# Layer 1's operands on VectorE in a fixed order, half its first values ahead of them, and flips two blocks ahead

## The chip, the cores and the metric

One core of a Trainium2 chip runs the kernel. The metric is the device time of one execution in microseconds, the median of the runs. TensorE (PE) multiplies, VectorE (DVE), ScalarE (ACT) and GpSimd (POOL) do the rest, SyncE (SP) issues the loads and stores.

## The reference

A trunk of two layers on 1024 tokens of width 1024, in float32, with pre-RMSNorm and residual adds. Layer 0 has global, windowed and memory heads; layer 1, which the change touches, is this:

```python
h = rmsnorm(x, norm_gain[l])
qc, kc, vc, qm, gate = split_cols(h @ w_in_odd[o], SPLIT_ODD)   # 1024, 1024, 1024, 512, 1536 columns
yc = neighborhood_attn(qc, kc, vc, rpb_c[o])    # 16 heads of 64; 8 x 16 window on the token grid
ym = memory_attn(qm, mk, mv)                    # 4 heads of 128; 256 memory tokens
y = jnp.concatenate([yc, ym], axis=-1) * jax.nn.silu(gate)
x = x + y @ w_out_odd[o]
```

## The kernel before

All large products run in a split form: each float32 operand is a high part and a low part (`x - high`), and a product is three matmuls (high-high, low-high, high-low). ScalarE copies out high parts, VectorE or GpSimd subtract to get low parts. Weights come by DMA into `wraw`, and `w_parts` (L1050) makes `wh` and `wl`. `either()` lets weights' low parts alternate between VectorE and GpSimd.

The stages follow each other in one program: preparation and layer 0, its output projection `out0`, then `front`, then layer 1's memory heads, its eight pairs of near heads, and `out1`. `front` (L1203) computes seven pairs of layer 1's projection columns (gates and memory queries) ahead. It uses a Strassen form: seven products of 12 matmuls of 128x512 for each pair of column tiles, 588 matmuls. Four of the seven need operands made of sums of blocks of the activations, `t1` to `t4` (4 tiles each, high and low). The half of the tokens that `out0` finishes last (`b12`, `b22`) is normalised inside the front: squares are summed in `out0` (`square`, L1111, GpSimd adding them through the tile `bt`), the sum goes through `rstd_cols` (matmuls L256, a chain of small VectorE operations, L229 to L234) and four flips (TensorE transposes) to one row per token, and VectorE scales `P` and `yb` tiles (L1243). The differences of L1226 and the low parts of L1228 and L1233 are shared between VectorE and GpSimd. For the weights, `sums` (L1336) makes four sums for each pair on GpSimd (VectorE for one pair). A pair's first two products are x (`begin`) and z (`second`); `finish` adds them, and `end` applies tanh for a gate. Five pairs start early, so x and z fill time while operands are made.

The order on each engine comes from a scheduler that runs through the program; `ahead(kind)` moves an operation up by the amount in `AHEAD`, `issue_after` holds one behind another, and `keep_in_program_order` pins VectorE's order for those operations that are marked.

In layer 1, `values` (L348) computes V for one half of the heads (8 head columns, group g) as a generator: 24 matmuls of 128x512 for each of 8 token blocks, in pieces of 12. `pull(n)` takes n pieces from the waiting generators and puts them between other work. Two such generators fill the memory heads (`mem_att`). In `near_head` (L922), a loop over 8 token blocks makes scores (L959, L960), the exponent and its normalisation (ScalarE L971 or GpSimd L973), and `values(j)` with flips (L110) and the products with V (L942); between flips and products it pulls `pulls` pieces of projection for the next pair (L215). The last pairs' gates are computed lazily, too, and `gated` (L389) multiplies a head's rows by them on GpSimd.

## Time and profile before

| | us |
|---|---|
| runs | 1574.67, 1576.52, 1577.83; median 1576.52 |
| profiled execution | 1580.0, of which the span from first to last instruction 1578.2 |
| busy: TensorE | 1502.0 (95%) |
| busy: VectorE, ScalarE, GpSimd | 1049.4, 838.6, 779.8 |
| front (first to last of its products) | 811.17 to 975.08 |
| memory heads with value matmuls | 987 to 1112 |
| near heads | 1130 to about 1440 |

The page's share for TensorE is a mean over stages. What a stage can lose is read in windows on it: its length less TensorE's busy time is idle time, and PEclk under 1.00 is time at the lower clock. A wait row names the tile that TensorE wanted and the engine that wrote it last. A "busy" matmul of 512 columns shows 0.39 us, but the next one starts 0.23 us later; the prices here go from start to start.

### The profile page before, as it was taken

What the parts mean: (1) busy time and instruction counts of PE and PEld (TensorE: products, weight loads), DVE (VectorE), ACT (ScalarE), POOL (GpSimd) and SP (SyncE); (2) the same over time, 40 slices, a digit from 0 to 9 for tenths busy, and PEclk for the clock granted to TensorE, in tenths of its full rate; (3) what the DMA queues carried; (4) which work ended last, traced back from release to release, by engine and by line L of the source; (5) the groups of instructions that cost most, each with busy time, mean ns of one, the idle gap of its engine ahead of it and who ended that gap; (6) DMA issues with size and microseconds to landing.
All of it is one profiled execution on the core that took longest, in us unless ns stands there. A gap on an engine that the chain in (4) does not pass through costs nothing. (4 is left out here: it accounts for less than half of the span.)

```text
span 1578.2 us, 24720 instructions
## 1 busy us (share of the span) xinstructions
PE 1502.0 (95%) x8082; PEld 1279.5 (81%) x8082; DVE 1049.4 (66%) x2210; ACT 838.6 (53%) x1890; POOL 779.8 (49%) x870
## 2 busy tenths in 40 slices
PE   6999999999999999999995999999999999998997
PEld 5899888888888788878874788877788888887786
DVE  7768677777776578766569654443477777776654
ACT  7644566556655456655445444343366666655442
POOL 2523455546563645432477654223266666643354
PEclk8999999999999999999998999999999999999998
DMA  9535332233232313387640344575556566767834
GB/s 349 181 102 159 98 103 102 66 129 101 83 125 75 126 65 107 100 277 243 195 167 34 134 160 150 177 239 174 169 180 185 176 201 203 221 188 264 272 119 135
DMA packets 163744, 249.83 MB, mean 158 GB/s; under 512 B 13856, under 2 KB 96032, under 8 KB 162592
## 3 DMA queue, kind: packets, MB, share of 16 engines
q1 hardware_dynamic: 162752, 247.52, 47.9%
q8 instruction: 64, 1.05, 0.3%
q10 hardware_dynamic: 864, 0.74, 0.2%
q14 instruction: 64, 0.52, 0.1%
HBM read 164.32 MB, written 74.45 MB: 151 GB/s over the span
## 5 line engine op out<-in xcount | busy, mean ns | idle before, releaser
L215 PE MATMUL pj<-H,wh 128*128 128x512 f32 x1248 | 418.4, 416 | 0.6 <-DVE vt L286 0.4
L102 ACT ACTIVATE ph<-tr 128x512 fp32r<-128x512 f32 (+2 forms) x336 | 180.6, 541 | 150.5 <-PE tr L110 144.5
L426 DVE TENSOR_TENSOR pl<-tr,ph 128x512 fp32r<-128x512 f32 (+2 forms) x336 | 205.7, 615 | 67.2 <-ACT ph L102 64.6
L215 PE MATMUL pj<-H,wl 128*128 128x512 f32 x624 | 247.9, 397 | 0.0
L215 PEld LDWEIGHTS pj<-H,wh 128*128 128x128 f32 x1248 | 215.0, 191 | 32.9 <-PE sa L560 0.8
L215 PEld LDWEIGHTS pj<-H,wl 128*128 128x128 f32 x624 | 118.0, 189 | 28.4
L1054 POOL TENSOR_TENSOR wl<-wraw,wh 128x384 fp32r<-128x384 f32 (+1 forms) x69 | 81.4, 1182 | 118.8 <-ACT wh L102 104.0
L102 ACT ACTIVATE wh<-wraw 128x384 fp32r<-128x384 f32 (+1 forms) x155 | 84.0, 549 | 92.0 <-PE tr L1100 17.3
L133 POOL TENSOR_TENSOR wl<-wraw,wh 128x512 fp32r<-128x512 f32 x86 | 112.1, 1306 | 22.0 <-ACT wh L102 14.5
L973 POOL TENSOR_SCALAR pn<-pn,st 128x384 f32<-128x384 f32 (+1 forms) x128 | 76.8, 602 | 90.8 <-DVE st L972 53.4
L110 PE MATMUL tr<-ident,P 128*128 128x128 f32 x752 | 117.5, 275 | 1.9 <-POOL P L583 1.8
L132 POOL TENSOR_SCALAR wh<-wraw 128x512 fp32r<-128x512 f32 x86 | 56.4, 656 | 123.5 <-PE pj L215 92.8
L880 POOL TENSOR_SCALAR P<-P,st 128x1024 f32<-128x1024 f32 x64 | 75.8, 1186 | 67.1 <-DVE st L879 67.0
L110 PEld LDWEIGHTS tr<-ident,P 128*128 128x128 f32 x752 | 90.4, 141 | 10.4 <-POOL P L583 3.0
L971 ACT ACTIVATE pn<-pn,st 128x384 f32<-128x384 f32 (+1 forms) x128 | 74.8, 585 | 36.2 <-DVE st L970 30.5
L878 ACT ACTIVATE P<-sa,st 128x1024 f32<-128x1024 f32 x64 | 71.5, 1118 | 41.6 <-DVE st L877 24.6
L877 DVE TENSOR_REDUCE st<-sa 128x1 f32<-128x1024 f32 x64 | 77.6, 1219 | 13.0 <-PE sa L873 11.9
L365 PE MATMUL pj<-k,H 128*128 128x512 f32 x256 | 84.4, 398 | 0.3 <-DVE ph L373 0.3
L702 PE MATMUL pj<-ah,H 128*128 128x256 f32 x384 | 72.9, 286 | 0.0
L110 PE MATMUL tr<-ident,pn 128*128 128x128 f32 x352 | 66.9, 275 | 4.9 <-POOL pn L973 4.4
L583 POOL TENSOR_SCALAR P<-P,st 128x384 f32<-128x384 f32 (+1 forms) x64 | 38.9, 625 | 59.9 <-DVE st L578 54.6
L967 DVE CUSTOM_DVE_ANT_0 pn<-s,bm 128x384 f32<-128x384 f32 x96 | 52.3, 555 | 22.6 <-PE s L960 10.0
(456 smaller groups left out, 4061.7 us busy)
## 6 DMA issues: line engine op xcount, KB each, us to landing
wraw<-w_o SPq DMA_DIRECT2D x62, 256.0 KB, 4.0
y<-sg SPq DMA_DIRECT2D x24, 512.0 KB, 2.9
y<-yb SPq DMA_DIRECT2D x24, 512.0 KB, 3.2
wraw<-s SPq DMA_DIRECT2D x64, 192.0 KB, 3.3
wraw<-w_e SPq DMA_DIRECT2D x44, 256.0 KB, 2.9
k<-k SPq DMA_DIRECT2D x36, 256.0 KB, 3.9
wraw<-w_mem SPq DMA_DIRECT2D x32, 256.0 KB, 4.4
v<-ph SPq DMA_DIRECT2D x32, 256.0 KB, 2.2
```

The source lines that it names most:

```text
L102: return self.nc.scalar.activation(out, in_, AF.Copy, scale=scale)
L110: self.turned = self.fence = self.nc.tensor.transpose(o, i, self.ident)
L133: (nc.gpsimd if self.wsplit[1] == "pool" else nc.vector).tensor_tensor(lf, raw, hf, op=OP.subtract)
L215: nc.tensor.matmul(a[:, :n], s[:, kt % UNIT, :], m, start=(kt == 0 and i == 0), stop=(kt == KT - 1 and i == 2))
L365: nc.tensor.matmul(p, x[kt][:, t], m, start=(kt + i == 0), stop=(kt == KT - 1 and i == 2))
L426: nc.vector.tensor_tensor(pl[:, :n], tr[:, :n], ph[:, :n], op=OP.subtract)
L702: self.last = nc.tensor.matmul(a[:, b * 256:(b + 1) * 256], x[kt][:, t], w, start=(kt + b + i == 0), stop=(kt == KT - 1 and i == 2), skip_ ...
L877: nc.vector.tensor_reduce(st[:, 0:1], s, axis=AX.X, op=OP.max, negate=True)
L880: self.normal = nc.gpsimd.tensor_scalar(pt, pt, st[:, 2:3], 0.5, op0=OP.mult, op1=OP.mult)
L971: nc.scalar.activation(o, o, AF.Exp, bias=st[:, 1:2], accum_out=st[:, 2:3])
L973: normal = nc.gpsimd.tensor_scalar(o, o, st[:, 3:4], 0.5, op0=OP.mult, op1=OP.mult)
L1054: engine.tensor_tensor(lf, raw, hf, op=OP.subtract)
```

## The change

1. In `front` every operand, sum and low part runs on VectorE; a wrapper `Pinned` keeps their program order. That order is written by hand in a string: `x` and `z` are products, `.` and a digit are steps of the operand maker, `V` is a piece of values. In the rest of the front, `more(n)` advances the operands by n steps.
2. `values_of_two` computes V for two head pairs instead of four, 128x256 each, two token blocks in one PSUM bank. The first half of group 0 runs in the front (`V`, 16 pieces of 12 matmuls; weights in the tiles of `t4`). The second half is the first filler of layer 1, then `values` for group 1 as before.
3. `finish` copies z on ScalarE and adds x on VectorE. The raw weights of a pair come in four DMAs into tiles of their own.
4. `near_head` runs ten rounds: scores of block b, flips of block b - 2, a pull, then the products with V of block b - 2. Pulls are 2 in each round (3 for the last pair before). Gate 7 lies in a tile of tag `k`. Evictions of values get the priority `evict`.

```diff
+class Pinned:
+    def __getattr__(self, name):
+        return lambda *a, **k: self.tc.keep_in_program_order(getattr(self.engine, name)(*a, **k))
...
+    def values_of_two(self, w, vd, tag, bank, out, pieces=1):
...
+                self.copy(h4, raw)
+                (nc.vector if pieces > 1 else nc.gpsimd).tensor_tensor(l4, raw, h4, op=OP.subtract)
+        yield
+        for b in range(0, 8, 2):
+            p = self.ps(bank[b // 2 % len(bank)])
+            for e in range(2):
...
+                for kt in range(KT):
+                    for i, (x, m) in enumerate(((0, hs), (0, ls), (1, hs))):
+                        self.last = nc.tensor.matmul(p[:, 256 * e:256 * e + 256], self.h[x][kt][:, t], m[kt // 2][:, kt % 2, :],
...
+                    if kt % 4 == 3 and (e == 0 or kt < KT - 1):
+                        yield
+            for e in range(2):
...
+                    self.copy(o[:, :, :, 0, :], src)
+                    self.vec.tensor_tensor(o[:, :, :, 1, :], src, o[:, :, :, 0, :], op=OP.subtract)
...
+            yield
...
-        for b in range(8):
+        def scores(b):
...
+        for b in range(10):
+            if b < 8:
+                scores(b)
+            if b > 1:
+                parts = flips(b - 2)
+            self.pull(pulls)
+            if b > 1:
+                values(b - 2, parts)
+            if b == 6:
                 close(0)
...
+        def operands():
...
+            for kt, x in enumerate(b12 + b22):
+                with self.ahead("norm"):
+                    pinned.scalar_tensor_tensor(x, x, self.gain[:, 8 + kt:9 + kt], rows, op0=OP.mult, op1=OP.mult)
+                yield from split(x, *(t[kt][:, 512:] for t in self.h))
+            yield from differences(((b11, b12, b11, t1),))
+            for op in sums_in_steps(first):
+                yield
+            yield from differences(((b11, b22, b11, t2), (b12, b22, b12, t3)))
+            t4.extend([self.st("t4", [128, 512], F32R) for _ in range(2)] for _ in range(4))
+            yield from differences(((b21, b11, b21, t4),))
...
+        def split(x, h, l):
+            with self.ahead("norm"):
                 self.copy(h, x)
+            yield
+            low.append((l, x, h))
+            if len(low) > 2:
+                low_part()
+                yield
...
-                return self.w_parts(raw, engine or self.either(), UNIT)
+                return self.w_parts(raw, engine or v, UNIT)
...
-                self.copy(c, x)
-                plus(c, z)
-                end(n1, 0, c)
+                self.copy(c, z)
+                e.tensor_tensor(c, c, x, op=OP.add)
+                end(n1, 0, c, e)
...
+        for i, kind in enumerate(plan):
+            if kind in "012345":
+                for _ in range(int(kind)):
+                    next(steps)
+                continue
...
-                self.front(wo, pairs, 5, (0, 1, 2, 5, 6, 3, 4), x1, rows1, dests)
+                v2 = self.values_of_two(wo[O_V:O_V + 2], vd[0], "t4", ("y", "pv"), "vt", 4)
+                self.front(wo, pairs, (0, 1, 2, 5, 6, 3, 4), v2, "x.x.V2V2V2V1V2V2V2V1x2z2V2V2V2V1V2V2V2V1x2z2x2z2z2z2", x1, rows1, dests)
...
-        self.waiting += [self.values(w[O_V:], vd, g) for g in range(2)]
+        self.waiting += [self.values_of_two(w[O_V + 2:O_V + 4], vd[1], "v", ("pj",), "ph"), self.values(w[O_V:], vd, 1)]
...
-                self.near_head(q[i], ks[i], v, i, bm[i], y, side, 2 if j < 7 else 3)
+                self.near_head(q[i], ks[i], v, i, bm[i], y, side, 2)
```

Where the order moves, shown at three places. In these rows a tile has its name and a running number; line numbers of the changed kernel are its own (L1324 is its product, L408 its `values_of_two`, L58 the wrapper `Pinned`, L1007 and L1008 the scores, L990 the products with V, L120 the flips).

TensorE, around the statistics; before, two products x precede the matmuls with `rows` (the sum of squares):

```order
L1274 MATMUL x_9345<-H_8869,wh_9348 128x512
L1274 MATMUL x_9345<-H_8861,wl_9349 128x512
L256 MATMUL pv_9364<-inv_d_67,rows_1679_8118 128x1 x4
L1274 MATMUL x_9385<-H_8858,wh_9388 128x512
L1274 MATMUL x_9385<-H_8866,wh_9388 128x512
```

After, one product x precedes them, and one follows:

```order
L1324 MATMUL x_9339<-H_8861,wh_9329 128x512
L1324 MATMUL x_9339<-H_8869,wh_9329 128x512
L1324 MATMUL x_9339<-H_8861,wl_9330 128x512
L266 MATMUL pv_9358<-inv_d_67,rows_1679_8118 128x1 x4
L1324 MATMUL x_9379<-H_8858,wh_9335 128x512
L1324 MATMUL x_9379<-H_8866,wh_9335 128x512
L1324 MATMUL x_9379<-H_8858,wl_9336 128x512
```

One product moved from ahead of the statistics to behind them. Behind that product and the flips come 8 pieces of values.

VectorE, behind the small operations; before, scaling (`gain`) alternates with the differences and the adds of finished products, while part of the work stands on GpSimd:

```order
L234 SCALAR_TENSOR_TENSOR rq_y_9372<-rq_t_9373,rq_y_9372 128x4
L1243 SCALAR_TENSOR_TENSOR P_8124<-P_8124,gain_65,tr_9404 128x512 x2
L1226 TENSOR_TENSOR P_8128<-P_8124,P_8128 128x512
L1243 SCALAR_TENSOR_TENSOR P_8125<-P_8125,gain_65,tr_9404 128x512
L1226 TENSOR_TENSOR P_8128<-P_8124,P_8128 128x512
L1297 TENSOR_TENSOR vt_9492<-vt_9492,pv_9473 128x512
L1228 TENSOR_TENSOR t_1926_9295<-P_8128,t_1925_9294 128x512
L1243 SCALAR_TENSOR_TENSOR P_8125<-P_8125,gain_65,tr_9404 128x512
L1226 TENSOR_TENSOR P_8129<-P_8125,P_8129 128x512
```

After, all of the low parts of `H` stand here, and evictions of values (`vt`) between them:

```order
L58 TENSOR_TENSOR wl_9395<-wraw_9392,wh_9394 128x512
L400 TENSOR_TENSOR t_1981_9412<-wraw_9425,t_1977_9408 128x512
L58 SCALAR_TENSOR_TENSOR P_8124<-P_8124,gain_65,tr_9398 128x512 x2
L58 SCALAR_TENSOR_TENSOR P_8125<-P_8125,gain_65,tr_9398 128x512
L58 TENSOR_TENSOR H_8866<-P_8124,H_8858 128x512
L58 SCALAR_TENSOR_TENSOR P_8125<-P_8125,gain_65,tr_9398 128x512
L58 TENSOR_TENSOR H_8867<-P_8124,H_8859 128x512
L58 SCALAR_TENSOR_TENSOR yb_8130<-yb_8130,gain_65,tr_9398 128x512
L58 TENSOR_TENSOR vt_9488<-y_9429,vt_9488 128x4x64
L58 TENSOR_TENSOR vt_9492<-y_9429,vt_9492 128x4x64
```

The low parts of the scaled tiles came over from GpSimd, and the differences moved behind them; `P_8128<-P_8124,P_8128` (the first tile of t1's difference) is the 19th operation behind the small ones, where it was the third.

TensorE, in the second head of a near pair; before, a piece of projection (`pj`) stands between flips (`tr`) and products with V in every round:

```order
L215 MATMUL pj_14302<-H_8863,wl_14185 128x512
L942 MATMUL pv_14147<-pl_14299,v_13357 128x128
L942 MATMUL pv_14148<-pl_14299,v_13357 128x256
L110 MATMUL tr_14374<-ident_63,pn_14319 128x128
L110 MATMUL tr_14374<-ident_63,pn_14345 128x128
L215 MATMUL pj_14302<-H_8864,wh_14184 128x512
```

After, the last rounds of the pair have none; scores of the next pair stand in their place:

```order
L990 MATMUL pv_14928<-pl_15094,v_14113 128x128
L990 MATMUL pv_14929<-pl_15094,v_14113 128x256
L990 MATMUL pv_14929<-ph_15124,v_14113 128x384
L1007 MATMUL s_15280<-k_14644,q_14648 128x384
L1008 MATMUL s_15280<-k_14645,q_14648 128x384
L120 MATMUL tr_15140<-ident_63,pn_15082 128x128
L120 MATMUL tr_15140<-ident_63,pn_15107 128x128
L990 MATMUL pv_14929<-pl_15125,v_14113 128x384
L1007 MATMUL s_15307<-k_14644,q_14648 128x384
L1008 MATMUL s_15307<-k_14645,q_14648 128x384
```

The pieces of projection moved to earlier rounds, and the flips stand further ahead of the products that use them.

## Rows read from the trace of the kernel before

**Rows 1.** Page, part 1: busy us, share, instructions of each engine.

```profile
PE 1502.0 (95%) x8082; PEld 1279.5 (81%) x8082; DVE 1049.4 (66%) x2210; ACT 838.6 (53%) x1890; POOL 779.8 (49%) x870
```

**Rows 2.** Windows: us, busy (x instructions) of five engines, PEclk, DMA share, GB/s.

```profile
820.50:825.00 4.50, 4.50 (x14) 3.06 (x13) 4.09 (x8) 0.00 (x0) 3.97 (x4) 0.62 0.95 335
...
861.00:872.00 11.00, 7.59 (x16) 5.08 (x17) 10.44 (x12) 3.30 (x6) 4.48 (x3) 0.50 0.18 57
888.00:975.08 87.08, 87.08 (x380) 71.45 (x381) 41.19 (x49) 35.73 (x63) 48.81 (x37) 1.00 0.41 142
811.17:975.08 163.91, 143.78 (x601) 114.27 (x600) 105.03 (x123) 71.43 (x126) 104.08 (x73) 0.95 0.34 120
```

**Rows 3.** Waits of TensorE, 811 to 975: us in total, times, longest us.

```profile
PE x L1274 <- DVE t L1228: 7.5, 2, 5.8
PE pv L1274 <- DVE vt L1297: 4.5, 2, 2.8
PE y L1274 <- DVE wl L1054: 3.3, 1, 3.3
PE pv L256 <- DVE rows L1465: 2.8, 1, 2.8
```

**Rows 4.** Timeline of GpSimd and VectorE: start, us, engine, line, operation, out<-in.

```profile
858.74 6.74 POOL L1226 TENSOR_TENSOR P<-P,P 128x512 f32<-128x512 f32 x4
...
862.60 1.74 DVE L1228 TENSOR_TENSOR t<-P,t 128x512 fp32r<-128x512 f32 x1
...
865.95 0.68 DVE L1054 TENSOR_TENSOR wl<-wq,wh 128x512 fp32r<-128x512 f32 x1
866.55 0.68 DVE L1297 TENSOR_TENSOR vt<-vt,pv 128x512 f32<-128x512 f32 x1
```

**Rows 5.** Timeline, last squares and sums on ScalarE, GpSimd, VectorE.

```profile
806.86 0.63 ACT L1114 ACTIVATE bt<-P 128x512 f32<-128x512 f32 x1 [3.46 <-DVE P L1109]
...
817.73 0.63 ACT L1114 ACTIVATE bt<-yb 128x512 f32<-128x512 f32 x1 [1.33 <-POOL vt L1116]
...
816.43 1.27 POOL L1116 TENSOR_TENSOR vt<-vt,bt 128x512 f32<-128x512 f32 x1
...
818.39 1.07 DVE L1465 TENSOR_TENSOR rows<-vt,bt 128x512 f32<-128x512 f32 x1 [6.33 <-ACT bt L1114]
...
820.87 1.14 DVE L229 TENSOR_SCALAR rq_i<-rq_v 128x4 int32<-128x4 int32 x1
...
824.76 0.16 DVE L232 TENSOR_TENSOR rq_t<-rq_y 128x4 f32<-128x4 f32 x1
```

**Rows 6.** Timeline of TensorE in the first stage: matmuls of 256 columns.

```profile
100.09 0.40 PE L702 MATMUL pj<-ah,H 128*128 128x256 f32 x2
...
101.87 0.40 PE L702 MATMUL pj<-ah,H 128*128 128x256 f32 x2
```

**Rows 7.** Groups of TensorE by line, 986 to 1112 us: busy, mean ns, idle before.

```profile
L365 PE MATMUL pj<-k,H 128*128 128x512 f32 x256 | 84.4, 398 | 0.3 <-DVE ph L373 0.3
L365 PE MATMUL pj<-v,H 128*128 128x512 f32 x128 | 50.5, 394 | 1.5 <-POOL v L358 1.5
```

**Rows 8.** Windows in the memory heads, columns as in rows 2.

```profile
1015.00:1044.00 29.00, 29.00 (x148) 24.35 (x147) 11.35 (x26) 10.71 (x31) 5.03 (x9) 1.00 0.53 182
1044.00:1075.00 31.00, 25.53 (x131) 19.34 (x130) 14.45 (x33) 14.62 (x43) 18.10 (x21) 1.00 0.62 210
```

**Rows 9.** Timeline in a memory head: last score, and its normalisation.

```profile
1016.21 0.28 PE L496 MATMUL s<-k,q 128*128 128x256 f32 x1
...
1019.18 0.94 POOL L515 TENSOR_SCALAR k<-k,st 128x256 f32<-128x256 f32 x2 [19.23 <-DVE st L513]
```

**Rows 10.** Timeline near 1430 us: GpSimd gating and a flip on TensorE.

```profile
1428.79 1.26 POOL L409 TENSOR_TENSOR sg<-yb,sg 128x512 f32<-128x512 f32 x1 [6.36 <-DMA sg<-y]
...
1433.10 0.48 PE L110 MATMUL tr<-ident,pn 128*128 128x128 f32 x1 [4.43 <-POOL pn L973]
```

**Rows 11.** Waits of TensorE, 1130 to 1440, columns as in rows 3.

```profile
PE s L959 <- DVE st L967: 3.8, 7, 0.7
```

More of the change, by code (lines that the diff above doesn't have):

```diff
@@ L934, in values @@
                           for b in range(b0, b1))
-            parts = self.p_parts(tr, (b1 - b0) * 128)
-            self.pull(pulls)
+            return self.p_parts(tr, (b1 - b0) * 128)
+        def values(j, parts):
+            b0, b1 = max(0, j - 1), min(8, j + 2)
             with self.ahead("pv"):
@@ L1201, in out_project, with front @@
                 list(done([t[:, :, cols] for t in c11 + c21], [sums[0][:, cols], sq[:, cols]], 512 + c, 256))
-    def front(self, w, pairs, early, order, x1, squares, dests):
+    def front(self, w, pairs, order, values, plan, x1, squares, dests):
         nc, tc = self.nc, self.tc
@@ new lines, in split, with differences @@
+        def split(x, h, l):
+            with self.ahead("norm"):
+                self.copy(h, x)
+            yield
+            low.append((l, x, h))
+            if len(low) > 2:
+                low_part()
+                yield
+        def differences(ops):
+            for dst, a, b, ts in ops:
+                for k in range(4):
+                    with self.ahead("norm"):
+                        pinned.tensor_tensor(dst[k], a[k], b[k], op=OP.subtract)
+                    yield from split(dst[k], *ts[k])
@@ L1313, in second @@
-        def second(j):
-            z = self.ps("pv")
-            ws = unit(self.wload(w[pairs[j][0]][:, 512:1024]), g)
-            with tc.issue_after(fence.ins):
-                product(z, ws, of_h(1, 0))
-            finish(xs[j], z, pairs[j][0], "vt")
-        def step():
-            with tc.issue_after(self.last.ins):
-                return next(steps)
+                self.copy(c, z)
+                e.tensor_tensor(c, c, x, op=OP.add)
+                end(n1, 0, c, e)
         def raw(j):
-            raw = self.st("wq", [128, 4, 512])
+            raw = [self.st("wq", [128, 512]) for _ in range(4)]
@@ new lines, in sums_in_steps, with sums @@
+        def sums_in_steps(ws):
+            s1, a11, a12, a21, a22 = ws
+            for o, a, b, op in ((s1, a21, a22, OP.add), (a21, a11, a21, OP.subtract), (a11, s1, a11, OP.subtract),
+                                (a12, a12, a11, OP.subtract)):
+                with self.ahead("w"):
+                    (pinned if ws is first else v).tensor_tensor(o, a, b, op=op)
+                yield
+        def sums(ws):
+            with self.ahead("w"):
+                ws = [self.st("wraw", [128, 512], pool=self.base, bufs=4)] + ws
+            list(sums_in_steps(ws))
+            return ws
@@ new lines, in front, with weights @@
+        first = [self.st("wq", [128, 512])] + raw(0)
+        steps = operands()
+        xs, parts = {}, deque()
+        todo = deque((k, i) for k in "xz" for i in range(plan.count(k)))
+        todo = deque((k, plan[:i].count(k)) for i, k in enumerate(plan) if k in "xz")
+        products = deque(todo)
+        def weights(e=pinned):
+            if todo:
+                k, j = todo.popleft()
+                c = 512 * (k == "z")
+                parts.append(unit(self.wload(w[pairs[j][0]][:, c:c + 512]), e))
@@ new lines, in front @@
+        weights(v)
+        weights(v)
+        self.last = self.vec = None
+        begun = 0
+        for i, kind in enumerate(plan):
[3 more added lines that the diff above has]
+                continue
+            with tc.issue_after(self.last.ins) if self.last else nullcontext():
+                if kind == "V":
+                    self.vec = pinned
+                    if not begun:
+                        next(values)
+                        begun = 1
+                    next(values, None)
+                elif kind == ".":
+                    next(steps)
+                else:
+                    k, j = products.popleft()
+                    if kind == "x":
+                        xs[j] = self.ps("x")
+                        product(xs[j], parts.popleft(), of_h(0, 0))
+                    else:
+                        z = self.ps(("pv", "tr")[j % 2])
+                        product(z, parts.popleft(), of_h(1, 0))
+                    weights()
+                    if kind == "z":
+                        finish(xs[j], z, pairs[j][0], "wq", pinned)
@@ L1374, in front, with more @@
             c22, c12, c21 = (self.st("P", [128, 512]) for _ in range(3))
-            e = v if j == 0 else None
-            product(y, unit(s1, e), t1)
+            def more(n):
+                for _ in range(n):
+                    next(steps, None)
+            product(y, unit(s1), t1)
+            more(4)
             with self.ahead("sink"):
                 self.copy(c22, y)
-            product(x, unit(a11, e), t2, False)
+            u = unit(a11)
+            more(4)
+            product(x, u, t2, False)
             with self.ahead("sink"):
                 self.copy(c12, x)
-            product(x, unit(a21, e), t3, False)
+            product(y, unit(a12), of_h(1, 1), False)
+            with self.ahead("sink"):
+                plus(c12, y)
+                end(n1, 1, c12)
+            u = unit(a21)
+            more(40)
+            product(x, u, t3, False)
             with self.ahead("sink"):
@@ L1386, in front @@
                 end(n2, 1, c22)
[L1387 to L1391 removed]
+            product(z, unit(a22), t4)
             with self.ahead("sink"):
```

149 lines of the change are left out of this document (50 added, 99 removed).

## The prediction

> **What bounds the kernel now.** I read the page's first part first: TensorE is busy 1502.0 of 1578.2 us [rows 1], so time is won only by giving it less to do, by closing its gaps, or by keeping its clock up. Up to 811.17 us, the end of layer 0's output projection, the instruction order of every engine is the same in both kernels, so only the rest can change. I cut the rest into stretches and looked for those where TensorE is not full. The stage "front", 811.17 to 975.08, is the poor one: 143.8 busy of 163.9 us, while from 888 on it runs without a gap, 380 matmuls in 87.08 us, 0.229 each [rows 2]. The front has 588 product matmuls (134.7 us at that price) and 13 small ones, for which I put 0.1 each, near the 0.119 of the smallest shape priced below: 136.0 together. So **27.9 us of the front are lost**. TensorE's waits name where: 7.5 for operands that VectorE makes (t), 4.5 for the sum in vt, 3.3 for a weight's low part, 2.8 for the sum of squares, 18.1 in all [rows 3]. Two stretches ran at the lower clock of 1.2 GHz for much of their time: 820.5 to 825 (14 matmuls in 4.5 us, mean clock 0.62) and 861 to 872 (16 in 11.0 us, 3.4 of them waits, mean 0.50) [rows 2]; against 0.229 each that cost about 1.3 and 3.9 us. Both lie behind waits.
>
> Why is VectorE late? Its low part at 862.60 took 1.74 us and the next, at 865.95, 0.68; what ended between is a group of four GpSimd subtractions, 6.74 us from 858.74, 1.69 each [rows 4]. So two subtractions, one on either engine, took 1.7 us; two on VectorE alone would take 1.2, by the 0.60 from the start at 865.95 to the next [rows 4]. The small operations behind the statistics show the same: 1.14 us for 4 columns while GpSimd works, 0.16 when it is silent [rows 5].
>
> The Trainium skill has a rule on this, page "SBUF — State Buffer", section "Who interferes with whom": a VectorE instruction with both inputs in SBUF contends with a GpSimd instruction that reads SBUF, and the shared ports are held for the whole instruction. The trace agrees in kind (1.74 against 0.68 us). Since after the change GpSimd is silent in the front, the rule changes nothing in the sum below.
>
> **The change, part by part.**
>
> *Operands on VectorE alone.* In the front GpSimd is left without an instruction. VectorE has some 206 operations there, 124 us at 0.60, against 159 us of TensorE work: enough, if it is never long behind.
>
> *Values in the front.* 192 matmuls of 128x256 move in (half of one of the two value groups). The shape is in the trace at 100 us: 15 in 1.78 us, 0.119 each [rows 6]. 192 x 0.119 = **22.8 us** onto TensorE.
>
> One rule speaks for less: the Trainium skill, "TensorE: Matmul & The Clock Gate", section "Back-to-back issue gap", gives columns / 2.4 GHz + 2.5 ns, 0.109 us here, an estimate of 21.0 us for the 192. The sum takes the measured 0.119; by the rule it would be 1.8 us lower, and as much higher in layer 1's fill for a part of the same shape, so the total is the same to 0.1.
>
> *What is left of the gaps.* I laid the new orders of the engines against each other by hand, at the trace's durations.
> - Start. The sum of squares is a chain of five links: each square waits for the addition before it, since both use the tile bt [rows 5]. Without GpSimd's low parts between, a link is 0.63 + 1.29 and some 0.15 of hand-over, 2.1 us: five from 806.9 [rows 5] and the last sum on VectorE end at about 816.9, where they ended at 819.5. But only one product now stands ahead of the statistics, not two, and it ends 12 x 0.229 = 2.75 after 811.17, at 813.9. So a wait of 3.0 us stays there, where 2.8 was. Behind it I expect the lower clock again, as at 820.5; one product and the small operations then bring the flips' end to about 822.8. Work of 24 x 0.229 + 1.3 = 6.8 us takes 11.6: **4.8 lost**, between 3 (clock kept) and 6.
> - Then come 8 calls of 12 value matmuls on the first four token blocks, which need nothing new (11.4 us, to 834.2), a product x and a product z (5.5, to 839.7), and values on the new columns, whose last tile is wanted 24 x 0.119 = 2.9 later, at 842.6. VectorE has 26 operations from the flips to that tile's low part (15.6 us) and waits about 4.7 us meanwhile, mostly in the finish for the end of z: 843.1, **0.5 short**.
> - For t1 to t4 the same count puts VectorE 1 to 2 us ahead each time, and from some 890 on a pair needs 15 to 19 operations (9 to 11 us) against 14 to 19 us of products. For what such a count misses I put **1.7** in sum. The lower bound is 0; the upper 7.5, the waits for t staying as they are [rows 3].
>
> Front: 136.0 + 22.8 + 7.0 = 165.8 against 163.9: **+1.9**, between -1.8 and +9. The moved work costs nearly nothing there, because it takes the place of 21 us of gaps.
>
> *Layer 1 without those values.* The 384 matmuls of 128x512 that fill between the memory heads [rows 7] cost 384 x 0.229 = 88.0 us. Left are 192 of 128x256 (22.8) and 192 of 128x512 (44.0): **-21.2**. This is the gain, and it counts in full where TensorE is full: 29.00 of 29.00 us in 1015 to 1044 [rows 8].
>
> *Thinner filler.* The first value generator is pulled there in pieces of 12 matmuls of 256 columns, 1.43 us instead of 2.75. A memory head's chain from score (1016.21) to the normalised row (1019.18 + 0.94) takes 3.9 us [rows 9], which a pull and the next scores no longer cover. A stretch without any filler (1044 to 1075) had 25.53 busy of 31.00 us, 5.5 lost [rows 8]. Lower bound 0, upper twice that, 11; I take **+2**, nearer to the full stretch, since the order still has filler between any two scores of a head.
>
> *Near heads.* Flips two blocks ahead cost no instruction. At 1433.10 a flip waited 4.43 us for GpSimd, which had stood 6.36 us before the gated rows at 1428.79 for a DMA [rows 10]. In the new order the flip's normalisation still stands behind these rows on GpSimd, but more TensorE work lies ahead of the flip, 13.7 us by count where about 15 are wanted: 1 us left, **-3.5**. Against it, 40 pulls for 32 token steps leave the last four rounds of a pair without filler: some 4.3 us of scores of the next heads, flips and values, in which VectorE and ScalarE set the pace. The kernel before has such waits of up to 0.7 us, 7 in all [rows 11]. From 0 to twice the longest for each of 7 pairs, 0 to +10; I take **+1.5**, since flips and scores run ahead. Near heads: -2.0.
>
> **Sum.** 1.9 - 21.2 + 2 - 2.0 = -19.3 on the profiled run's 1580.0 us: 1560.7. That run stood 3.5 us above the median of the three, so the forecast is 1557.2, said as **1557**.
>
> **The rivals.**
> 1. *The memory heads lose their cover* (chance 0.17): +11 instead of +2, 1566. For it: a chain of 3.9 us over pulls of 1.43. Against: at 1015 to 1044 the cover was ample, and 192 matmuls of fill remain for the first two heads.
> 2. *The pairs' tails* (0.11): +10 instead of +1.5, 1566. For it: without filler VectorE paces every block, and there are seven such places. Against: flips run two blocks ahead.
> 3. *The front's gaps stay* (0.06), because something else binds, late weights above all (their DMAs queue on SP behind others). Then the values only add: +22.8 - 21.2 + 2 - 2.0 = +1.6, 1578, within 0.2%.
> 4. *The pinned VectorE queue blocks; slower than before* (0.09). In the one fixed order a pair of evictions or a finish stands ahead of low parts that TensorE wants, and itself waits for TensorE and for ScalarE's copy. There are 8 pairs of evictions and 5 finishes, 13 such places. If each costs as much as the longest wait for a sum in vt, 2.8 us of the 4.5 [rows 3], that is 36 us: 1593. It decides at 19.3 / 13 = 1.5 us a place. Against: in the hand count only one of them shows.
>
> **How the numbers follow.** The forecast has 0.57. Its front alone reaches from -3.7 to +7 about it, the other terms from -3.5 to some +4: 1550 to 1568. Rivals 1 and 2 stand inside, both together at 1574 outside. As the clock at the start and the near heads may give more than counted I go a little lower, so the range is **1547 to 1571**; outside are rivals 3 and 4 and the far corners. A measurement of this kernel tells some 0.2% (3.2 us) from no change. Faster 0.85, within 0.2% 0.06, slower 0.09.
>
> **What would show it.** A front of about 166 us with GpSimd silent and VectorE's operations at 0.60 to 0.68; the wait for the statistics still near 3 us and a low clock behind it, but none in 855 to 872; TensorE's wait for t under 2 us; value matmuls at 0.119; the memory heads some 19 us shorter; no wait over 2 us at the last gate's GpSimd rows. Wrong would be a wait of TensorE on VectorE of over 3 us elsewhere in the front (rival 4), on weights' DMAs (rival 3), over 10 us of waits in the memory heads (rival 1), or over 1 us at each pair's end (rival 2).

## The result, and the profile after

The changed kernel takes 1550.32 us (median of runs from 1546.54 to 1553.06) against 1576.50 before: a ratio of 0.983, with a 95% interval of 0.981 to 0.986. In a later set of runs the same kernel gave 0.982 (0.980 to 0.984). The forecast was 1557 with a range of 1547 to 1571, faster. The sign and the range held, but the gain is 26 us where 19 were forecast, and its parts are quite other than forecast.

The first part of the page of the changed kernel, as [rows 1]. TensorE does less by 6.2 us and its idle time falls from 76 to 53 us:

```profile
span 1548.4 us, 25122 instructions
...
PE 1495.8 (97%) x8274; PEld 1284.8 (83%) x8274; DVE 1062.1 (69%) x2277; ACT 841.0 (54%) x1890; POOL 675.3 (44%) x803
```

I cut both traces at the first matmul of each stage. Windows of the changed kernel (us, busy and instructions of PE, PEld, DVE, ACT, POOL, then PEclk, DMA share, GB/s): front, memory heads, and all from the first near score to the end; the front's row answers to the last of [rows 2].

```profile
812.21:984.04 171.83, 164.45 (x793) 136.58 (x792) 119.86 (x202) 78.74 (x139) 6.98 (x6) 0.98 0.39 134
...
995.03:1114.76 119.73, 114.39 (x657) 97.32 (x655) 51.98 (x106) 48.09 (x130) 37.42 (x52) 1.00 0.63 211
...
1114.76:1548.40 433.64, 422.33 (x2243) 361.57 (x2243) 303.06 (x872) 254.58 (x594) 243.20 (x320) 0.99 0.62 198
```

The same two last stages of the kernel before:

```profile
986.07:1128.23 142.16, 135.49 (x657) 110.05 (x655) 55.28 (x116) 52.91 (x142) 39.96 (x54) 1.00 0.62 203
...
1128.23:1578.20 449.97, 427.12 (x2243) 364.91 (x2243) 303.06 (x872) 254.07 (x594) 249.16 (x320) 0.98 0.60 191
```

So the front is **7.9 us longer** (forecast: 1.9 longer), the memory heads **22.4 shorter** (forecast 19.2), and near heads with the last projection **16.3 shorter** (forecast 2.0), with the same 2243 matmuls in it. That is 30.8; the program ahead of the front, the same in both, ended 1.0 us later here, so the two profiled executions differ by 29.8 us (the medians by 26.2, since the profiled execution before stood 3.5 us above its median). The front starts between 806 and 812 us in the runs below, so their profiles are compared by stages, from the first matmul of the front on. Each stage length is of one execution; how far it repeats is told with the experiments.

The waits of TensorE in the front, as [rows 3] (total us, times, longest):

```profile
PE pv L266 <- DVE rows L1536: 2.7, 1, 2.7
PE pv L1324 <- ACT P L112: 1.9, 2, 1.0
PE x L1324 <- ACT P L112: 1.7, 1, 1.7
PE y L408 <- DVE H L58: 0.9, 1, 0.9
```

The waits for t, vt and wl are gone: 7.2 us are left, where the four rows of [rows 3] have 18.1. What the forecast said of the start is there, too. The timeline of TensorE at the statistics and the flips:

```profile
817.85 1.82 PE L266 MATMUL pv<-inv_d,rows 128*128 128x1 f32 x8 [2.73 <-DVE rows L1536]
819.54 1.20 PE L1324 MATMUL x<-H,wh 128*128 128x512 f32 x2
...
823.52 1.05 PE L1324 MATMUL x<-H,wh 128*128 128x512 f32 x2
...
824.76 0.60 PE L120 MATMUL tr<-ident,rq_y 128*128 128x128 f32 x4
825.12 5.99 PE L408 MATMUL y<-t,H 128*128 128x256 f32 x48
830.94 5.92 PE L408 MATMUL pv<-t,H 128*128 128x256 f32 x48
```

Two matmuls take 1.05 there where they take 0.62 at full speed: the lower clock (1.2 GHz) stood behind the wait of 2.73 as it stood behind that of 2.8 before, and ended with the flips. The windows from the front's start to the first value and behind it show the granted clock, 0.74 and then 1.00:

```profile
812.21:825.12 12.91, 10.18 (x38) 8.14 (x36) 7.12 (x21) 5.68 (x10) 2.83 (x2) 0.74 0.73 245
825.12:836.80 11.68, 11.68 (x100) 11.68 (x98) 9.38 (x16) 5.32 (x10) 0.00 (x0) 1.00 0.24 81
```

### The profile page after: what moved, and what is told of

Same layout as the page of the kernel before. It is cut to its first block, busy times and chain, and to the rows that moved or that the text cites. A ratio compares the mean times of both kernels' runs of the same rounds, so it can differ in the third digit from the quotient of the medians.

```text
span 1548.4 us, 25122 instructions
## 1 busy us (share of the span) xinstructions
PE 1495.8 (97%) x8274; PEld 1284.8 (83%) x8274; DVE 1062.1 (69%) x2277; ACT 841.0 (54%) x1890; POOL 675.3 (44%) x803
## 4 chain that ended last, share of the span: by engine, by line
PE 86%; DVE 4%; DMA 3%; ACT 2%; issue 1%; POOL 1%; SPq 0%; DVEq 0%; ACTq 0%; POOLq 0%
PE pj L225 27%; PE tr L120 9%; PE pv L951 4%; PE x L1324 4%; PE pj L1154 3%; PE sa L1154 3%; PE pv L990 3%; PE tr L1154 3%; PE pj L748 3%; PE s L1154 2%; PE y L1324 2%; PE pj L375 2%; PE pv L1324 2%; PE sa L918 2%; PE sa L919 2%; PE pv L1154 2%
## 5 line engine op out<-in xcount | busy, mean ns | idle before, releaser
L120 PE MATMUL tr<-ident,P 128*128 128x128 f32 x752 | 117.4, 275 | 2.0 <-POOL P L629 2.0
L1108 POOL TENSOR_TENSOR wl<-wraw,wh 128x384 fp32r<-128x384 f32 x56 | 62.8, 1122 | 110.6 <-ACT wh L112 88.8
L120 PEld LDWEIGHTS tr<-ident,P 128*128 128x128 f32 x752 | 90.3, 141 | 10.5 <-POOL P L629 3.0
L1108 DVE TENSOR_TENSOR wl<-wraw,wh 128x384 fp32r<-128x384 f32 (+1 forms) x64 | 48.9, 763 | 27.9 <-ACT wh L112 27.8
L1015 DVE CUSTOM_DVE_ANT_0 pn<-s,bm 128x384 f32<-128x384 f32 x96 | 53.2, 555 | 19.9 <-PE tr L120 14.3
L951 PE MATMUL pv<-ph,va 128*128 128x256 f32 x256 | 66.8, 285 | 0.0
L951 PE MATMUL pv<-pl,va 128*128 128x256 f32 x256 | 66.1, 283 | 0.0
```

Of the source, the lines that this page charges most:

```text
L120: self.turned = self.fence = self.nc.tensor.transpose(o, i, self.ident)
L951: nc.tensor.matmul(o[:, :256], v[:, c + k, kv, :], part[:, k * 256:(k + 1) * 256], start=(c + k == 0 and part is parts[0]), stop=(c + k == ...
L1108: engine.tensor_tensor(lf, raw, hf, op=OP.subtract)
```

## The experiments

All kernels below are timed against the kernel before on the same chip; the ratio is given with its interval. The stage lengths (us) come from their traces, cut at the same first matmuls:

| kernel | front | memory heads | near heads to end | ratio |
|---|---|---|---|---|
| before | 163.9 | 142.2 | 450.0 | 1 |
| changed | 171.8 | 119.7 | 433.6 | 0.983 (0.981 to 0.986) |
| changed, again | 172.2 | 122.5 | 433.6 | 0.982 (0.980 to 0.984) |
| before, new near heads | 163.8 | 141.7 | 434.0 | 0.989 (0.987 to 0.991) |
| changed, old near loop | 171.5 | 121.3 | 441.5 | 0.986 (0.984 to 0.987) |
| changed, 32 pulls | 170.4 | 120.8 | 440.7 | 0.986 (0.984 to 0.987) |
| changed, flips one ahead, 40 pulls | 170.4 | 119.2 | 437.1 | 0.983 (0.981 to 0.985) |
| changed, last gate in sg | 170.4 | 121.5 | 442.2 | 0.988 (0.985 to 0.990) |
| changed, no values in the front | 163.3 | 143.2 | 434.9 | 0.990 (0.987 to 0.992) |
| changed, low parts on GpSimd | 170.7 | 120.2 | 434.7 | 0.981 (0.979 to 0.982) |
| changed, front shared | 181.2 | 120.7 | 435.8 | 0.987 (0.986 to 0.989) |
| changed, two products first | 178.7 | 119.9 | 433.7 | 0.984 (0.982 to 0.985) |
| changed, sums of squares | 169.8 | 120.1 | 434.7 | 0.982 (0.980 to 0.984) |
| changed, low parts and sums | 170.6 | 120.4 | 434.1 | 0.980 (0.979 to 0.982) |

**The changed kernel again** gives the scatter.

> The changed kernel itself, on the same chip as the three below: 0.983 of the kernel before, about 1551 to 1553. Its stages by first instructions should repeat within 1 us: front 171.8, memory heads 119.7, near heads 299.7, last projection 133.9; only the part ahead of the front, which is the same program in all, varies by some us from one execution to another.

In these two the front repeats to 0.4 us and the near heads to 0.1; the memory heads differ by 2.8, more than expected. The table as a whole shows more scatter than the pair:

- Six traces (the changed kernel twice, the old near loop, 32 pulls, 40 pulls, the last gate in sg) have the same order of instructions in the front. Their fronts are 170.4 to 172.2 us. Up to the first value five of them take 11.3 us and the first one 12.9, where the 8 small matmuls behind the wait took 1.82 us (1.02 to 1.15 in the others) and the granted clock was 0.74 (0.85 in the changed kernel again). From the first value to the last all six take 29.7.
- Eleven traces have the new filler in the memory heads: 119.2 to 122.5 us.
- Nine traces have the new near heads whole: 433.6 to 435.8 us to the end.

A difference inside these ranges is not read below.

### The near heads: loop, pulls and the gate's tile

**The old loop in the changed kernel**, and **the new near heads alone** in the kernel before:

```diff
-        for b in range(10):
-            if b < 8:
-                scores(b)
-            if b > 1:
-                parts = flips(b - 2)
-            self.pull(pulls)
...
+        for b in range(8):
...
+            if b:
+                values(b - 1)
...
-                self.near_head(q[i], ks[i], v, i, bm[i], y, side, 2)
+                self.near_head(q[i], ks[i], v, i, bm[i], y, side, 2 if j < 7 else 3)
```

> The changed kernel with the near heads' loop of before (flips one block ahead, 2 pulls a round, 3 in the last pair). Theory A, from the two traces: the near heads and the start of the last output projection gained 10.6 + 5.5 = 16 us by the new loop, so this kernel takes about 1550 + 16 = 1566, and its trace has a wait of over 3 us for pn near the last gate and one of over 2 us for H in the last projection. Rival B, the forecast's term: the loop is worth 2 to 4 us (1553), and the rest comes from where the stages now start.

> The kernel before with the near heads' new loop and the last gate in a tile of tag k, and nothing else of the change. Theory A: 16 us less than before, about 1560, with near heads free of waits. Rival B: 2 to 4 us less, about 1573.

The second agrees with theory A: 450.0 to 434.0 us, as short as in the whole change, and 17 us by time (1578.81 to 1561.67). The new near heads owe nothing to the front. The first agrees with neither theory: undoing the loop costs 7.9 us by trace (0.986 against 0.983 and 0.982, some 3 to 6 us, by time), not 16, and more than rival B's 2 to 4. Its window from the first near score to the end:

```profile
1113.61:1555.10 441.49, 423.52 (x2243) 362.81 (x2243) 302.79 (x872) 255.59 (x594) 249.18 (x320) 0.99 0.63 194
```

Of the two waits that theory A named, the one for pn is there, at 2.7 us:

```profile
PE tr L120 <- POOL pn L1019: 2.7, 1, 2.7
```

The one for H in the last projection, which the kernel before has, is not:

```profile
PE pj L1100 <- ACT H L102: 2.6, 1, 2.6
```

One thing in this kernel was not undone: the last gate's tile. Its own run:

```diff
-                self.lazily(lambda: self.gate(w, O_G + 7, "k"), sgs.append)
+                self.lazily(lambda: self.gate(w, O_G + 7), sgs.append)
```

> The changed kernel with the last gate in a tile of tag sg, as before, of which there is one. If the tile counts, that gate can only be made once the gate before it has been used, so its work comes late, TensorE waits near 1400 us, and near heads and last projection are 2 to 6 us longer. If it doesn't, both stay at 299.7 and 133.9.

It costs 8.6 us by trace (0.988 against 0.983 and 0.982, some 7 to 9 us, by time), more than the 2 to 6 expected. By the traces loop 7.9 and tile 8.6 make 16.5; the whole is 16.0 to 16.3. The window of the last 40 us of near heads with the tile of tag sg:

```profile
1376.32:1416.32 40.00, 36.68 (x195) 31.30 (x195) 29.18 (x93) 24.83 (x64) 18.06 (x25) 0.96 0.63 203
```

The first matmul behind it on TensorE's timeline:

```profile
1416.32 0.72 PE L1128 MATMUL pj<-k,wh 128*128 128x512 f32 x2 [0.82 <-DVE sg L431]
```

The same place in the changed kernel, without idle time:

```profile
1374.48:1414.48 40.00, 40.00 (x225) 34.66 (x223) 30.67 (x100) 26.57 (x66) 21.43 (x30) 1.00 0.71 229
```

With one sg tile the last gate's result waits until the gate before it has been used, and 30 matmuls fewer fit in these 40 us. GpSimd's last operation on the gate before, and ScalarE's first write of the last gate, with the tile of tag sg:

```profile
1409.78 1.60 POOL L458 TENSOR_TENSOR yb<-sg,yb 128x512 f32<-128x512 f32 x1
...
1414.95 0.60 ACT L430 ACTIVATE sg<-pj 128x512 f32<-128x512 f32 x1 [1.97 <-DMA H<-x]
```

In the changed kernel that write goes to the tile of tag k. It comes 7.1 us behind ScalarE's last write of the gate before (1397.94); with the tile of tag sg it comes 16.1 behind it (1398.86):

```profile
1405.02 0.60 ACT L430 ACTIVATE k<-pj 128x512 f32<-128x512 f32 x1 [1.92 <-PE pj L225]
```

How the 8.6 us divide between waits, clock and order isn't settled.

**The loop in two parts**: flips two ahead with the old number of pulls, and the new number with flips one ahead.

```diff
-            self.pull(pulls)
             if b > 1:
+                self.pull(pulls)
                 values(b - 2, parts)
```

> The changed kernel with flips two blocks ahead, but a pull only in the eight rounds that have values, so 32 pulls for a pair as before, not 40. Theory G (the lag gives the gain): near heads 300 us, as in the changed kernel. Rival H (the gain is that scores and exponents of the next heads come forward, because the filler is used up two rounds earlier): near heads 304 to 311 us, with the waits for st and for pn of the kernel before, and 1555 to 1562.

```diff
-        for b in range(10):
+        for b in range(9):
...
-                parts = flips(b - 2)
-            self.pull(pulls)
+                parts = flips(b - 1)
+            self.pull(pulls + (b in (0, 1)))
```

> The changed kernel with flips one block ahead as before, but 40 pulls for a pair (one more in each of the first two of nine rounds). Rival H, which the run with 32 pulls supports: the gain of the near heads comes from the filler being used up earlier, so here near heads are 300 to 301 us and the last projection 134 to 135 us, about 1551. Theory G (the lag gives it): near heads 304 to 306 and 1555 to 1557.

With 32 pulls the stage is 7.1 us longer than in the changed kernel, with flips one ahead and 40 pulls 3.4. Neither lands quite where it was expected: to the first matmul of the last projection the near heads take 303.0 us with 32 pulls (G: 300, H: 304 to 311), and 301.5 with flips one ahead (H: 300 to 301, G: 304 to 306). Rival H holds for the larger part. Eight more pulls give 7.1 us with flips two ahead and 4.4 with flips one ahead; the lag gives 0.8 with 32 pulls and 3.4 with 40. By time the pulls show (1554.95 against 1549.45 on the same chip) and the lag doesn't: 40 pulls with flips one ahead give 0.983, the changed kernel 0.983 and 0.982. So it is the pulls that count; that the lag adds to them is in one trace only, 1.3 us outside the scatter of the near heads. One thing isn't separated: in the last pair the old loop had 48 pulls, where the run with 32 has 32.

The waits in the run with 32 pulls show where the time goes (TensorE, total, times, longest):

```profile
PE s L1007 <- DVE st L1015: 4.3, 8, 0.7
```

This is the wait of [rows 11], 8 times, about once for each pair: a score wants a bank that VectorE is still reading. With 40 pulls a pair's projections are used up four rounds before its end, the next pair's scores move up into the unfilled rounds, and the wait falls to 0.3 us in all. These 4.0 us are the greater part of the 5.9 by which TensorE is idle longer with 32 pulls. Windows of 200 us in the middle of the near heads, for the run with 32 pulls:

```profile
1150.98:1350.98 200.00, 197.22 (x1101) 171.91 (x1101) 148.25 (x493) 128.38 (x314) 126.85 (x175) 1.00 0.65 196
```

For the changed kernel:

```profile
1154.76:1354.76 200.00, 199.99 (x1113) 173.07 (x1112) 149.27 (x498) 129.86 (x320) 122.88 (x177) 1.00 0.63 197
```

And for the kernel before:

```profile
1168.23:1368.23 200.00, 196.80 (x1097) 171.29 (x1098) 148.29 (x491) 128.25 (x315) 126.35 (x174) 1.00 0.63 195
```

### The front: what the values cover, and who makes the operands

**No values in the front**, both groups filling the memory heads as before (of the first changed line only the string is shown):

```diff
-"x.x.V2V2V2V1V2V2V2V1x2z2V2V2V2V1V2V2V2V1x2z2x2z2z2z2"
+"x.x.22212221x2z222212221x2z2x2z2z2z2"
...
+        self.waiting += [self.values(w[O_V:], vd, g) for g in range(2)]
```

> The changed kernel without values in the front: both groups of values fill the memory heads as before, and the front has its operands on VectorE in the same fixed order, without the 16 pieces of value matmuls. Theory A: the pieces cover the time in which VectorE makes operands, so without them TensorE waits for operands instead: the front loses 23 us of matmuls but gets most of them back as waits (front 160 to 170 us), the memory heads are 22 us longer, and the sum is 1563 to 1570. Rival C: VectorE alone has closed the gaps by being faster, and the values were only carried from one stage to the other: front 149 us, sum about 1550.

Theory A. The window of its front:

```profile
810.16:973.44 163.28, 146.78 (x602) 116.91 (x600) 114.53 (x190) 73.96 (x127) 6.97 (x6) 0.94 0.36 122
```

Two of TensorE's waits there (total, times, longest):

```profile
PE x L1324 <- DVE wl L58: 10.2, 2, 5.9
PE pv L266 <- DVE rows L1536: 2.7, 1, 2.7
```

Taking 192 matmuls out shortens the front by 8.5 us only, and the memory heads become 23.5 longer: the values cost 8.5 us in the front for what cost 23.5 in layer 1, a gain of 15. Against all six traces with that front the gain is 12 to 17, and by time, 0.990 against 0.983 and 0.982, it is 10 to 12. And with VectorE alone in the fixed order but no values, the front is 163.3 us, where it was 163.8 with shared engines (before with new near heads). **By itself the move to VectorE gains nothing**, together with what came with it in the front (one product ahead of the statistics, the new `finish`, four DMAs for a pair's weights, none of which has a run of its own): its 10.2 us of waits for wl stand where the 7.5 for t stood.

**Low parts on GpSimd**, and **the front shared** as nearly as before:

```diff
-                pinned.tensor_tensor(*low.popleft(), op=OP.subtract)
+                nc.gpsimd.tensor_tensor(*low.popleft(), op=OP.subtract)
```

> The changed kernel with the low parts of the operands (28 subtractions of 128x512 in the front) on GpSimd instead of VectorE; the rest of the order stays. Theory E (two engines side by side cost each other as the trace of before showed): VectorE's operations beside them go from 0.60 to about 1.7 us, 28 x 1.1 = 31 us more of VectorE time against 17 us that it gives up, so the operands come later and the front grows by 5 to 25 us, 1557 to 1575. Rival F: the front has its cover from the values now, VectorE gives up 17 us of work, and the time stays within 2 us of the changed kernel.

Theory E fails here: the front is 170.7 us, inside the scatter, and the ratio no worse (24 subtractions moved, not 28). VectorE's operations did get slower beside them, though. Groups of GpSimd and VectorE in its front (count, busy us, mean ns):

```profile
L1298 POOL TENSOR_TENSOR t<-P,t 128x512 fp32r<-128x512 f32 x16 | 23.9, 1510 | 23.4 <-ACT t L112 17.7 <-PE pv L1324 5.7
...
L58 DVE TENSOR_TENSOR wl<-wraw,wh 128x512 fp32r<-128x512 f32 x8 | 7.7, 960 | 0.0
L58 DVE TENSOR_TENSOR P<-yb,P 128x512 f32<-128x512 f32 x8 | 6.5, 835 | 0.0
```

The second of VectorE's groups takes 685 ns each in the changed kernel, 835 here. That the values are what covers it is argued, not shown: low parts on GpSimd without values were not run. Groups of VectorE in the changed kernel's front:

```profile
L1370 DVE TENSOR_TENSOR wq<-wq,wq 128x512 f32<-128x512 f32 x12 | 8.2, 688 | 0.1
...
L58 DVE TENSOR_TENSOR P<-yb,P 128x512 f32<-128x512 f32 x8 | 5.5, 685 | 0.0
```

The Trainium skill ("SBUF — State Buffer", section "Who interferes with whom") has it that a VectorE instruction with two inputs in SBUF contends with a GpSimd instruction that reads SBUF. The trace agrees in direction (835 against 685 ns on VectorE, beside GpSimd's 1510), but here it cost the kernel nothing.

```diff
-                return self.w_parts(raw, engine or v, UNIT)
+                return self.w_parts(raw, engine or self.either(), UNIT)
...
-                    (pinned if ws is first else v).tensor_tensor(o, a, b, op=op)
+                    (pinned if ws is first else nc.gpsimd).tensor_tensor(o, a, b, op=op)
```

> The changed kernel with the front shared between VectorE and GpSimd again: operands' low parts and the weights' sums (but the first pair's) on GpSimd, weights' low parts on either in turn. Theory E, in its last form (VectorE alone is needed): the front grows by over 5 us. Rival F, which the run with the low parts on GpSimd supports: the values cover the operands whatever engine makes them, the front is 170 to 174 us and the time within 2 us of the changed kernel, about 1551.

With these two edits on top (the weights' sums and half of their low parts on GpSimd) theory E is right and rival F wrong: the front is 9.4 us longer. Its waits, where the changed kernel has none for a weight:

```profile
PE y L1324 <- POOL wl L1108: 2.2, 1, 2.2
...
PE y L1324 <- ACT wh L112: 1.6, 1, 1.6
PE x L1324 <- ACT wh L112: 1.2, 1, 1.2
```

Its sums on GpSimd, to be read against the row of L1370 above:

```profile
L1370 POOL TENSOR_TENSOR wq<-wq,wq 128x512 f32<-128x512 f32 x12 | 18.3, 1532 | 0.2
```

So of "VectorE alone" it is the weights that matter, not the operands: a weight's sums (four subtractions and additions, one after the other, 1.53 us each on GpSimd against 0.69 on VectorE), its high part and its low part are one chain in front of each product, and the values don't lie over that: the last value starts at 847.18 us in this run, the first of these waits ends at 881.93. The weights alone on GpSimd, with the operands on VectorE, were not run.

**Two products first**, as the kernel before had it (the string alone; its later products change places, too):

```diff
-"x.x.V2V2V2V1V2V2V2V1x2z2V2V2V2V1V2V2V2V1x2z2x2z2z2z2"
+"xx.x.V2V2V2V1V2V2V2V1z2x2V2V2V2V1V2V2V2V1z2x2z2z2z4"
```

> The changed kernel with the plan's start as before the change: two products x ahead of the statistics and one behind them, the later products keeping the cover of the operands. Theory A: the 2.7 us wait for the sum of squares and the low clock behind it (6.1 us lost ahead of the first values) go in large part, since 2.75 us of work stand over the wait: 3 to 5 us less than the changed kernel, about 1546. Rival D: VectorE's small operations behind the statistics and the operands set the pace, so the time comes back as a longer wait for H: within 1 us of the changed kernel.

Neither theory: the front is 6.9 us longer (6.5 to 8.3 against the six traces; by time, 0.984 against 0.983 and 0.982, it isn't told from the changed kernel). The wait for the sum of squares is gone, and others stand in its place, none of them for H:

```profile
PE y L1324 <- ACT P L112: 4.8, 1, 4.8
PE tr L120 <- DVE rq_y L244: 3.2, 1, 3.2
PE pv L1324 <- DVE vt L58: 1.9, 1, 1.9
```

The start itself lost less. Up to the first value it takes 13.5 us with one product more in it, so 4.0 are lost (36 x 0.229 + 1.3 = 9.5 us of work), where the changed kernel lost 6.1 in its first trace and 4.5 in the five others. The time goes behind the first value, at the waits for vt (837) and P (879).

The wait for rq_y has its cause in VectorE's timeline. The first small operation stands behind the low parts of the values' weights (L400), which wait for their copies, and a further one stands in the middle of the chain:

```profile
815.87 0.69 DVE L400 TENSOR_TENSOR t<-wraw,t 128x512 fp32r<-128x512 f32 x1 [0.81 <-ACT t L112]
816.48 0.15 DVE L269 TENSOR_SCALAR rq_v<-pv 128x4 f32<-128x4 f32 x1
...
819.26 0.69 DVE L400 TENSOR_TENSOR t<-wraw,t 128x512 fp32r<-128x512 f32 x1 [0.84 <-ACT t L112]
819.87 0.15 DVE L243 SCALAR_TENSOR_TENSOR rq_t<-rq_t,rq_v 128x4 f32<-128x4 f32 x1
820.06 0.16 DVE L244 SCALAR_TENSOR_TENSOR rq_y<-rq_t,rq_y 128x4 f32<-128x4 f32 x1
```

The wait for P is three engines deep. Timelines of VectorE and ScalarE: a weights' sum waits for its DMA, and the high part in ScalarE's queue waits for the sum. The copy that frees TensorE's bank y stands behind that high part, and then waits 0.52 us more for an operation of VectorE (t) that stands behind the same sum:

```profile
876.19 0.69 DVE L1370 TENSOR_TENSOR wraw<-wq,wq 128x512 f32<-128x512 f32 x1 [1.53 <-DMA wq<-w_o]
...
876.98 0.63 ACT L112 ACTIVATE wh<-wraw 128x512 fp32r<-128x512 f32 x1 [2.19 <-DVE wraw L1370]
878.12 0.60 ACT L112 ACTIVATE P<-y 128x512 f32<-128x512 f32 x1 [0.52 <-DVE t L58]
```

How much of the 4.8 us is the DMA's isn't settled; the wait for it that shows is 1.53. In the changed kernel ScalarE's queue makes the wait of 1.7 us for P in the same way: the copy stands behind a weight's high part and an operand's, which waited 1.09 and 1.11 us for VectorE:

```profile
878.83 0.64 ACT L112 ACTIVATE wh<-wraw 128x512 fp32r<-128x512 f32 x1 [1.09 <-DVE wraw L1370]
880.57 0.63 ACT L112 ACTIVATE t<-P 128x512 fp32r<-128x512 f32 x1 [1.11 <-DVE P L58]
881.11 0.58 ACT L112 ACTIVATE P<-x 128x512 f32<-128x512 f32 x1
```

This wait is 1.2 to 2.4 us in the six traces with that front.

**The sums of squares** on VectorE for the last three additions, and **both** this and the low parts on GpSimd:

```diff
-                nc.gpsimd.tensor_tensor(sums[0], sums[0], sq, op=OP.add)
+                (nc.vector if k > 3 else nc.gpsimd).tensor_tensor(sums[0], sums[0], sq, op=OP.add)
```

> The changed kernel with the last three additions of each sum of squares in the output projections on VectorE instead of GpSimd. The five links of squares and additions ahead of the front should shorten by three times 1.29 - 0.60, 2 us, so the sum of squares is ready some 2 us earlier, TensorE's wait for it falls from 2.7 to about 1 us, and the lower clock behind it goes or shortens: 2 to 5 us less than the changed kernel. Rival I: the last square waits for the last product's addition, not for the one before it, or VectorE's queue delays the addition: no change.

> The changed kernel with the operands' low parts on GpSimd and the last additions of the squares on VectorE. By the two single runs the front should be 168 to 169 us (170.7 and 169.8 apart, 172 in the changed kernel, their waits at different places), and the time 1545 to 1548, a little under the changed kernel. If the two hang on the same wait: 170 to 171.

The wait for the sum of squares falls from 2.7 to 1.6 us:

```profile
PE pv L266 <- DVE rows L1536: 1.6, 1, 1.6
```

The stretch up to the first value is 10.1 us, 1.2 less than the 11.3 of five of the six traces. The front as a whole, 169.8, is 0.6 below the shortest of the six, which isn't clear of their scatter; by time, 1548.82 against 1549.45, it isn't told from the changed kernel, so the 2 to 5 us expected are not shown. Both edits together gave 1546.65 us and 0.980, the lowest of all, but with a front of 170.6. The parts do shorten (9.6 us up to the first value, 28.7 from the first to the last, where the six have 29.7), but from the last value on the front takes 132.3 us, where the six have 129.3 to 131.2. The interval overlaps the changed kernel's, so no version is shown to beat it.

## Why the prediction was right, and where its sum was off

- **Direction and range** held, in part by luck. The main term was right: layer 1 loses 21.2 us of value matmuls, by trace 21.1 of busy time (135.49 to 114.39), and the front had gaps for most of them. The run without values shows the exchange itself, 8.5 against 23.5 us. But the near heads, forecast at -2.0, gave as much again: alone they take the kernel before from 1578.81 to 1561.67, so the direction would have held with no value moved. In the sum, a front 6.0 worse than forecast stands against near heads 14.3 and memory heads 3.2 better. The forecast's own terms reached down to 1550, and the 1550.32 measured lie at that end.
- **The front** was mis-sized: +1.9 forecast, +7.9 measured, and +6.5 to +8.3 over the six traces of that order, inside its bounds of -1.8 and +9 (the lower comes out as -1.6 by its own terms). The start was counted about right: 4.8 lost were forecast, 4.5 stand in five traces and 6.1 in the first, 1.3 more, where the lower clock came earlier. In the first trace 0.4 more are the tile of H (0.9, counted 0.5), 0.4 the values at 0.121 instead of 0.119 (5.82 us for 48), and 1.9 the waits for P (3.6, against 1.7 for all that was missed). The counts on record follow VectorE's queue, and these waits are for ScalarE's copies. Some 2 us have no name in the wait rows, in that trace and in the others; they lie behind the last value.
- **VectorE alone as the reason** was half wrong. The prediction took the gaps to be caused by contention, with the price of [rows 4] (1.74 against 0.68 us). The price is real, but without values the front keeps its length on one engine, and with values the operands may stay on GpSimd. What the runs leave for VectorE is the weights' chain.
- **Thinner filler** (+2) cost nothing: idle time in the memory heads fell from 6.7 to 5.3 us, and in all eleven traces they are at least 19.7 us shorter than before, more than the 19.2 forecast. So rival 1 didn't come.
- **The near heads** are the step that failed most: -2.0 forecast, -16.3 measured, 11.5 of it idle time of TensorE and 4.8 busy time, in which the same 2243 matmuls are done. The -3.5 counted only the wait at [rows 10]. Left out were the stretch behind it in the last projection (2.64 us of wait for H at 1484 and a granted clock of 0.91 from 1480 to 1500; this wait doesn't come back when the loop alone or the tile alone is undone) and the gate's tile, of which the part on the change said nothing more than its name. And the +1.5 for the pairs' tails had the wrong sign: the rounds without filler are where the next pair's scores went, and the 200 us in the middle of the near heads have no idle time left. The waits of [rows 11] were read as a cost that stays, and they were part of the gain: 3.8 us before, 0.3 after. So rival 2 didn't come.
- **The lower clock** at the start, named for 820 to 825, came as said; none came in 855 to 870 (PEclk 1.00).
- **Rivals 3 and 4** didn't come in the changed kernel, but both mechanisms, a late weight and a blocked VectorE queue, show in the waits of the run with two products first.

## What to carry to other kernels

Work that needs nothing new is worth most where operands are being made: it pays for its place with the gaps that it fills (8.5 us of front for 23.5 of layer 1 here), and more than a faster way to make the operands does. Before a filler's end is called a loss, look at what the order puts in the empty rounds, and before a wait is charged to an engine, follow that engine's queue back: a bank's copy on ScalarE was late in part for a DMA two engines away. A single-buffered result (the gate's tile, 8.6 us) can cost as much as a loop.

## What the runs showed that I had not expected

In the run with two products first, a chain of 12 small VectorE operations of 0.16 us took from 816.48 to 820.22 us. One subtraction of 0.69 us stood in its middle and waited 0.84 for a copy, so 1.45 of these 3.74 us lie between two small operations: in an engine's one order, a cheap chain is as late as what is queued inside it. The changed kernel has two such subtractions inside the chain, which wait for nothing, and takes 3.30 us for it.

The program up to the front is the same in twelve of the fourteen rows of the table (the two with sums of squares on VectorE change it), and it ended between 805.95 and 812.21 us in their profiled executions, a scatter wider than most effects measured here. Stages cut at the same instructions repeat better, but not to half a microsecond: 1.8 us in the front, 3.3 in the memory heads, 2.2 from the near heads to the end. The stretch from the first value to the last repeats to 0.1 us, so a short stretch, cut close around what an edit touches, tells more than a whole stage.
